# The lane of the other half's mixer is stepped at 1.15 pieces a step instead of 3

## The chip, the cores and the metric

The kernel runs on one core of one Trainium2 chip. The metric is the device time of one execution in microseconds; lower is better. All values are float32, and the large products run as three passes over numbers split into two parts of reduced mantissa (`float32r`).

## The reference

The reference is a decoder trunk of two layers over 1024 tokens of width 1024. Each layer has a mixer of three parallel head groups, a channel MLP and a gated per-layer embedding:

```python
xn = rmsnorm(h, attn_norm_g)
z = xn @ w_in
za, zq, zk, zv, zc = split(z)
ya = chunk_gmlp(za, ...)             # gated MLP over chunks of 128 tokens
yb = swa_sink_attention(q, k, zv)    # 8 query heads, 2 kv heads, window 128
yc = s5_ssm(zc, ...)                 # state space groups, scanned over time
y = concat([rmsnorm(ya), rmsnorm(yb), rmsnorm(yc)])
h = h + y @ w_out
h = h + square(relu(rmsnorm(h) @ w_ff1)) @ w_ff2     # D_FF = 4096
gate = sigmoid(rmsnorm(h) @ w_ple_gate)
h = h + gate * (p_i @ w_ple_proj)
```

## The kernel before

The 1024 tokens are cut into two halves of 512 (half 0 and half 1). Every product has 512 tokens as its moving side and 128 channels as its stationary side; a column block with 8 blocks of depth takes 8 times 3 passes = 24 matmuls. Weights come by DMA in float32 (512 KB each) and are split into a high part by ScalarE (line 104) and a low part by VectorE (line 105) before TensorE can use them; `Ring` loads them ahead of use, two tiles ahead for the MLP's ring (three buffers), one ahead for the mixer's ring (two buffers).

The main work is `window(l, h)`, once for each layer and half, in the order (0,0), (0,1), (1,0), (1,1): the MLP in 8 chunks of 512 hidden channels, then the 8 gate products of the embedding. A chunk has 4 up products (24 matmuls each, line 359 through `cm`; eviction by lines 1344 to 1348 into the tile `A`), then 8 down products of 12 matmuls each, added to `H` in `f2` (line 1333). In the last chunk `f2` also sums squares and makes the split input `x` for the gates (lines 329, 89, 90). After it `rstd_wide` makes the norm `rbc` (matmul line 288, a chain of VectorE and ScalarE steps on lines 289 to 297, PSUM bank "o", of which there is one), and the gates' evictions (line 1390) need it. The gates may use six banks ("mm" two, "s" two, "x", "p") before the first must be free again.

While the window of one half is written, a second generator, the lane, writes the mixer of the other half: `project` (z products: token part line 710, channel part through `cm` into bank "s"), `attention`, `ssm`, `gmlp` and `mix_out` (8 column blocks through `cm` into bank "s", added to `H` on line 1310, then its own `rstd_wide` and the split of the next MLP's input `x`). A piece is what the lane's generator does up to its next `yield`. `main` runs the window's own generator, and each 12 matmuls of it make a step: `tick` adds the lane's rate to an account and runs one piece for each whole unit in it. Two more ticks stand by hand in the first pair of down products of each chunk. So a chunk has 8 + 2 + 6 = 16 steps, the 8 gates have 16, and a window has 144; 120 of them stand before `until` in the last chunk, where all lanes are run on until the other half's `attention` and `ssm` are written. After the window `finish` writes what is left of the lane.

From the generators, a lane of `mix_lane` has 25 pieces in `project`, 42 or 43 in `attention` (half 0 or 1), 34 in `ssm`, 18 in `gmlp` and 18 in `mix_out`: 137 or 138. The lane in the first window is `left_lane`, of which `attention`, `ssm`, `gmlp` with the preparation of layer 1, and `mix_out` fall there; it has no `project`. The last window has no lane.

The order in which the pieces are written is not the order in which an engine runs them. The kernel leaves the order on each engine to the compiler's scheduler, which simulates the program, and at each point takes, of the instructions that it holds to be ready on an engine, the one that was written first. Each engine then runs its instructions in the order so fixed. The rate of a lane is therefore its precedence: a lane written at 3 pieces a step stands, as a whole, ahead of all of the MLP from the third chunk on.

Of the kernel before, what the change touches and what calls it, by code (L numbers as in the profile page):

```python
# [38 lines left out]
PASSES = ((0, 0), (1, 0), (0, 1))  # L39


RATE, RATE0, RATEL = 3.0, 2.0, 3.0


class Ring:
# [17 lines left out]
class Trunk:  # L63
# [1415 lines left out]
    def run(self):  # L1479
        self.setup()  # L1480
        zws, self.zw = ExitStack(), None
        self.zw = self.pool(zws, "zw", 4, side=self.side(0), reuse_waits="tile")
        xs, xp = self.stage("xin", 0)
        left = self.lane(self.left_lane(), RATEL)
        for _ in self.first_x(0, xp, left):
            pass
        x1 = self.lane(self.first_x(1, xp))
        gen = self.project0()
        z0 = self.lane(gen)
        self.until(lambda: x1[3] and ("zq", 0, 0) in self.flags)  # L1490
        xs.close()
        self.until(lambda: {"zg", "rotary"} <= self.flags)
        zws.close()
        self.lanes.remove(z0)
        pzs = ExitStack()
        self.zpools.append(self.pool(pzs, "pz", 2, side=self.side(0), reuse_waits="tile"))
        self.lane(self.gmlp(0, 0, 0, "x", [("attn", 0, 0)]), RATE0)
        self.until(lambda: True)
        self.lane(self.attention(0, 0, 0), RATE0)
        self.main(gen)  # L1500
        self.main(self.embed())
        self.until(lambda: {("attn", 0, 0), ("gm", 0, 0)} <= self.flags)
        self.zpools.pop()
        pzs.close()
        self.finish(self.lane(self.mix_out(0, 0, self.fring, "mm", 3)))
        seq = [(l, h) for l in range(DEPTH) for h in range(2)]
        nxt = left
        for i, (l, h) in enumerate(seq):
            self.window(l, h, self.stages(*seq[i + 1]) if i + 1 < len(seq) else set())
            if i + 1 < len(seq):  # L1510
                self.finish(nxt)
            if i + 2 < len(seq):
                nxt = self.lane(self.mix_lane(*seq[i + 2]), RATE)
# [30 lines left out]
```

## Time and profile before

| | |
|---|---|
| median of 3 runs | 2381.09 us |
| profiled execution: its own time | 2385.95 us |
| profiled execution: span | 2384.2 us |
| TensorE matmul busy | 2325.3 us (98%) |
| TensorE weight load busy | 1885.4 us (79%) |
| VectorE busy | 1552.8 us (65%) |
| ScalarE busy | 1027.8 us (43%) |
| granted TensorE clock, mean | 0.99 |

The runs shown are 2380.5, 2381.09 and 8480.06 us; the median is used. Busy times are unions of the instructions of one engine; a matmul's end is modelled, so neighbouring matmuls overlap in the records and their spacing is read from their starts.

### The profile page before, as it was taken

What the parts mean: (1) busy time and instruction counts of PE and PEld (TensorE: products, weight loads), DVE (VectorE), ACT (ScalarE), POOL (GpSimd) and SP (SyncE); (2) the same over time, 40 slices, a digit from 0 to 9 for tenths busy, and PEclk for the clock granted to TensorE, in tenths of its full rate; (3) what the DMA queues carried; (4) which work ended last, traced back from release to release, by engine and by line L of the source; (5) the groups of instructions that cost most, each with busy time, mean ns of one, the idle gap of its engine ahead of it and who ended that gap; (6) DMA issues with size and microseconds to landing.
All of it is one profiled execution on the core that took longest, in us unless ns stands there. A gap on an engine that the chain in (4) does not pass through costs nothing.

```text
span 2384.2 us, 29265 instructions
## 1 busy us (share of the span) xinstructions
PE 2325.3 (98%) x10941; PEld 1885.4 (79%) x10941; DVE 1552.8 (65%) x2700; ACT 1027.8 (43%) x1787; POOL 5.4 (0%) x15
## 2 busy tenths in 40 slices
PE   7998899999999999999999999999999999999998
PEld 5886687788788887777888888777888887888887
DVE  7877767675966765676585774676657674444455
ACT  7427646433334443553342543464334343322333
POOL 0000000000000000000000000000000000000000
PEclk9998999999999999999999999999999999999999
DMA  8663632253553335324443344522534334333333
GB/s 244 188 203 119 208 99 64 80 173 106 145 156 102 111 125 155 95 78 140 123 135 124 98 145 124 145 72 76 166 105 135 124 97 134 97 96 94 94 97 98
DMA packets 403558, 295.94 MB, mean 124 GB/s; under 512 B 66668, under 2 KB 376024, under 8 KB 401624
## 3 DMA queue, kind: packets, MB, share of 16 engines
q1 hardware_dynamic: 403416, 294.07, 41.1%
q8 instruction: 86, 1.41, 0.3%
q14 instruction: 56, 0.46, 0.1%
HBM read 250.48 MB, written 43.54 MB: 123 GB/s over the span
## 4 chain that ended last, share of the span: by engine, by line
PE 83%; DMA 7%; DVE 5%; ACT 3%; issue 2%; SPq 1%; ACTq 0%; DVEq 0%
PE mm_ps L359 43%; PE x_ps L359 20%; PE s_ps L359 8%; DMA st<-in_w_in 2%; DVE w L105 2%; PE s_ps L710 1%; PE po L1259 1%; PE pss L1201 1%; ACT w L104 1%; PE p_ps L359 1%; DMA st<-in_w_out 1%; PE p_ps L947 1%; DMA yu<-ye 1%; PE pt L1238 1%; SPq L98 1%
## 5 line engine op out<-in xcount | busy, mean ns | idle before, releaser
L104 ACT CAST w<-st 128x1024 fp32r<-128x1024 f32 x364 | 387.9, 1067 | 853.1 <-PE mm_ps L359 430.0
L359 PE MATMUL mm_ps<-x,w 128*128 128x512 f32 x2904 | 708.4, 396 | 7.9 <-ACT x L89 4.2
L359 PEld LDWEIGHTS mm_ps<-x,w 128*128 128x128 f32 x2904 | 544.5, 190 | 133.0 <-issue 10.1
L105 DVE TENSOR_TENSOR w<-st,w 128x1024 fp32r<-128x1024 f32 x364 | 448.5, 1234 | 202.6 <-ACT w L104 191.6
L359 PE MATMUL mm_ps<-A,w 128*128 128x512 f32 x2016 | 500.8, 392 | 2.5 <-DVE H L1333 2.5
L359 PEld LDWEIGHTS mm_ps<-A,w 128*128 128x128 f32 x2016 | 375.7, 188 | 85.4 <-DVE H L1333 4.9
L359 PE MATMUL x_ps<-A,w 128*128 128x512 f32 x1056 | 272.8, 393 | 4.1 <-DVE H L1333 4.1
L359 PE MATMUL x_ps<-x,w 128*128 128x512 f32 x1104 | 272.2, 394 | 0.0
L359 PE MATMUL s_ps<-x,w 128*128 128x512 f32 x1056 | 252.4, 391 | 4.8 <-DVE w L105 2.6
L359 PEld LDWEIGHTS x_ps<-x,w 128*128 128x128 f32 x1104 | 205.6, 188 | 45.6 <-issue 3.4
L359 PEld LDWEIGHTS s_ps<-x,w 128*128 128x128 f32 x1056 | 198.1, 188 | 49.1 <-DVE w L105 4.0
L359 PEld LDWEIGHTS x_ps<-A,w 128*128 128x128 f32 x1056 | 196.5, 188 | 51.0 <-DVE H L1333 8.3
L1333 DVE TENSOR_TENSOR H<-H,mm_ps 128x512 f32<-128x512 f32 x168 | 113.2, 683 | 84.2 <-PE mm_ps L359 83.3
L1344 DVE SCALAR_TENSOR_TENSOR r<-mm_ps,rbc 128x512 f32<-128x512 f32 x88 | 60.7, 690 | 119.2 <-PE mm_ps L359 119.2
L710 PE MATMUL s_ps<-w,x 128*128 128x512 f32 x384 | 101.3, 404 | 4.1 <-ACT x L89 2.6
L1333 DVE TENSOR_TENSOR H<-H,x_ps 128x512 f32<-128x512 f32 x88 | 60.2, 684 | 68.8 <-PE x_ps L359 68.2
L1348 DVE TENSOR_TENSOR A<-q,A 128x512 fp32r<-128x512 f32 x128 | 87.8, 686 | 6.8 <-ACT q L1347 6.6
L710 PEld LDWEIGHTS s_ps<-w,x 128*128 128x128 f32 x384 | 73.6, 194 | 20.8 <-ACT x L89 3.0
L1346 ACT ACTIVATE A<-r 128x512 fp32r<-128x512 f32 x128 | 80.2, 627 | 8.1 <-DVE r L1344 7.9
L1347 ACT ACTIVATE q<-r 128x512 f32<-128x512 f32 x128 | 78.9, 617 | 0.0
L1224 ACT ACTIVATE pr<-pr,anm,hf 128x128 f32<-128x128 f32 x128 | 61.6, 485 | 17.4 <-DVE anm L1221 17.4
L89 ACT ACTIVATE x<-H,gT 128x512 fp32r<-128x512 f32 x80 | 53.7, 711 | 13.5 <-PE s_ps L359 7.7
(386 smaller groups left out, 2112.3 us busy)
## 6 DMA issues: line engine op xcount, KB each, us to landing
st<-in_w_ff SPq DMA_DIRECT2D x256, 512.0 KB, 4.1
st<-in_w_out SPq DMA_DIRECT2D x32, 512.0 KB, 4.1
st<-in_w_ple_gate SPq DMA_DIRECT2D x32, 512.0 KB, 4.1
st<-in_w_in SPq DMA_DIRECT2D x18, 512.0 KB, 4.4
p<-par SPq DMA_DIRECT2D x8, 1024.0 KB, 8.5
pj<-pjz SPq DMA_DIRECT2D x32, 256.0 KB, 2.2
H<-hs SPq DMA_DIRECT2D x4, 2048.0 KB, 7.9
pj<-pj SPq DMA_DIRECT2D x32, 256.0 KB, 3.4
```

Source lines behind the costliest of these rows:

```text
L89: self.S.activation(hi, x, AF.Copy, scale=g)
L98: self.Q.dma_start(sv[:, :, c0:c1], src)
L104: self.S.copy(hi, src)
L105: self.V.tensor_tensor(lo, src, hi.bitcast(F32), ALU.subtract)
L359: self.T.matmul(ps, w[:, i, k, c0:c0 + P], X[:, j, k, :], start=(start and n == 0), stop=(stop and n == last))
L710: T.matmul(pss[b], X[:, j, 2 * s + kk, c], w[:, i, kk, :], start=(s == 0 and kk == 0 and n == 0), stop=(s == 3 and kk == 1 and n == 2))
L1224: S.activation(pr[:, i], pr[:, i], AF.Exp, bias=nm[:, i:i + 1], scale=f[:, i:i + 1], accum_out=den[:, i:i + 1])
L1333: V.tensor_tensor(H[:, m], H[:, m], ps, ALU.add)
L1344: V.scalar_tensor_tensor(r, ps, 0.0, self.R[h][1], ALU.max, ALU.mult)
L1346: S.activation(A[:, 0, m], r, AF.Square)
L1347: S.activation(q, r, AF.Square)
L1348: V.tensor_tensor(A[:, 1, m], q, A.bitcast(F32)[:, 0, m], ALU.subtract)
```

## The change

One rate is changed and one is added. `RATE`, the rate of `mix_lane` in the windows (0,1) and (1,0), goes from 3.0 to 1.15. The lane of the first window, created with `RATEL` = 3.0 and used at 3.0 so far, is set to the new `RATEW` = 1.25 before the first window is written. `RATE0` and `RATEL`, and with them the part before the first window, stay. The setting of the scheduler stays.

```diff
-RATE, RATE0, RATEL = 3.0, 2.0, 3.0
+RATE, RATEW, RATE0, RATEL = 1.15, 1.25, 2.0, 3.0
...
         seq = [(l, h) for l in range(DEPTH) for h in range(2)]
         nxt = left
+        nxt[1] = RATEW
         for i, (l, h) in enumerate(seq):
             self.window(l, h, self.stages(*seq[i + 1]) if i + 1 < len(seq) else set())
```

No instruction is added or removed by it, and no tile or buffer changes its size.

## Rows read from the trace of the kernel before

**Rows 1.** The page: busy time of the engines, and the granted clock in 40 slices

```profile
PE 2325.3 (98%) x10941; PEld 1885.4 (79%) x10941; DVE 1552.8 (65%) x2700; ACT 1027.8 (43%) x1787; POOL 5.4 (0%) x15
...
PEclk9998999999999999999999999999999999999999
```

**Rows 2.** Busy time by stretch: before the windows, then the four windows

```profile
core 0: us, PE busy (x) PEld busy (x) DVE busy (x) ACT busy (x) POOL busy (x), PEclk, DMA share, GB/s
0.00:338.00 338.00, 306.17 (x1525) 245.40 (x1525) 250.71 (x658) 188.06 (x410) 2.51 (x12) 0.96 0.61 184
338.00:842.10 504.10, 499.01 (x2375) 403.25 (x2375) 359.63 (x592) 222.97 (x383) 0.95 (x1) 0.99 0.39 115
842.10:1405.30 563.20, 557.03 (x2620) 452.37 (x2619) 369.46 (x602) 242.84 (x409) 0.96 (x1) 1.00 0.40 120
1405.30:1967.30 562.00, 557.40 (x2636) 452.90 (x2635) 369.70 (x599) 241.24 (x408) 0.95 (x1) 1.00 0.39 118
1967.30:2384.20 416.90, 405.73 (x1792) 331.45 (x1790) 203.26 (x253) 132.67 (x178) 0.00 (x0) 0.99 0.34 101
```

**Rows 3.** Busy time by stretch of 25 us: starts of lanes, attention, the lone MLP

```profile
350.00:375.00 25.00, 21.81 (x104) 18.41 (x103) 19.91 (x40) 17.07 (x43) 0.00 (x0) 0.86 0.25 74
925.00:950.00 25.00, 22.05 (x96) 17.35 (x96) 20.23 (x38) 10.07 (x16) 0.00 (x0) 1.00 0.59 156
950.00:975.00 25.00, 22.80 (x98) 18.57 (x99) 11.03 (x16) 8.39 (x14) 0.00 (x0) 0.93 0.49 149
1000.00:1025.00 25.00, 25.00 (x135) 19.41 (x134) 18.30 (x43) 15.12 (x44) 0.00 (x0) 1.00 0.29 84
2050.00:2075.00 25.00, 25.00 (x112) 20.70 (x111) 11.78 (x14) 6.23 (x7) 0.00 (x0) 1.00 0.35 106
```

**Rows 4.** Chain that ended last, in order of time: start, us, what (lone MLP)

```profile
2096.34 5.44 PE mm_ps L359 x24
```

**Rows 5.** Timeline of TensorE where lanes start: start, us, instruction [idle before <-releaser]

```profile
358.72 0.66 PE L1188 MATMUL pq<-identr,qst 128*128 128x128 f32 x4 [1.79 <-ACT kT L1122]
360.06 1.32 PE L1201 MATMUL pss<-kT,qt 128*128 128x256 f32 x8 [0.68 <-ACT qt L1191]
362.86 2.08 PE L1201 MATMUL pss<-kT,qt 128*128 128x256 f32 x8 [0.73 <-ACT qt L1191]
...
925.96 5.96 PE L359 MATMUL s_ps<-x,w 128*128 128x512 f32 x25 [1.00 <-DVE hss L701]
933.33 5.50 PE L359 MATMUL s_ps<-x,w 128*128 128x512 f32 x23 [1.41 <-DVE w L105]
939.62 0.47 PE L359 MATMUL s_ps<-x,w 128*128 128x512 f32 x1 [0.57 <-DVE z L742]
964.75 0.77 PE L1120 MATMUL pk<-identr,kst 128*128 128x128 f32 x4 [2.20 <-DVE kst L1117]
...
1500.20 5.53 PE L359 MATMUL s_ps<-x,w 128*128 128x512 f32 x23 [1.20 <-DVE w L105]
1506.59 0.47 PE L359 MATMUL s_ps<-x,w 128*128 128x512 f32 x1 [0.63 <-DVE z L742]
1530.54 0.66 PE L1120 MATMUL pk<-identr,kst 128*128 128x128 f32 x4 [1.25 <-DVE kst L1117]
```

**Rows 6.** Line 359 alone, by stretch: project, then up to mix_out, two windows

```profile
842.10:955.30 113.20, 67.53 (x281) 51.80 (x279) 1.00 0.48 143
955.30:1286.30 331.00, 292.20 (x1224) 228.38 (x1224) 0.99 0.37 113
1405.30:1522.20 116.90, 72.58 (x304) 56.30 (x302) 1.00 0.49 145
1522.20:1864.40 342.20, 300.80 (x1271) 235.95 (x1271) 1.00 0.37 111
```

**Rows 7.** Timelines of TensorE and VectorE at the end of window (1,0)

```profile
1924.80 1.02 PE L288 MATMUL o_ps<-nacc,onesr 128*128 128x512 f32 x2
1942.91 1.02 PE L288 MATMUL o_ps<-nacc,onesr 128*128 128x512 f32 x2
1956.02 5.60 PE L359 MATMUL p_ps<-x,w 128*128 128x512 f32 x24
...
1928.17 0.74 DVE L90 SCALAR_TENSOR_TENSOR x<-H,gT,x 128x512 fp32r<-128x512 f32 x1
1954.49 0.69 DVE L1390 TENSOR_TENSOR gt<-p_ps,rbc 128x512 f32<-128x512 f32 x1
```

**Rows 8.** Timeline of VectorE at the end of window (0,1): the lane's last split

```profile
1341.66 0.76 DVE L90 SCALAR_TENSOR_TENSOR x<-H,gT,x 128x512 fp32r<-128x512 f32 x1
```

**Rows 9.** Timeline of TensorE inside windows: waits for the MLP's own eviction

```profile
597.47 3.02 PE L359 MATMUL x_ps<-A,w 128*128 128x512 f32 x12 [1.15 <-DVE H L1333]
1718.96 5.76 PE L359 MATMUL mm_ps<-A,w 128*128 128x512 f32 x24 [1.19 <-DVE H L1333]
```

## The prediction

> **What bounds the kernel now.** I read first the busy times of the page, then the same by stretch with a boundary at each window, then the stretches of 25 us inside the windows, and where one of those is not full, the timeline of TensorE. The reader is to see the same thing at each level: TensorE has work nearly all of the time. It is busy for 98% of the span, VectorE for 65%, ScalarE for 43% [rows 1]. In the four windows it is idle for 5.1, 6.2, 4.6 and 11.2 us [rows 2]; the last of these has no lane, so the change can't reach it. Since ends of matmuls are modelled, busy time alone does not say that TensorE is at its peak, so I take a stretch in which the MLP runs alone: 112 matmuls in 25 us, 24 of them in 5.44 us, or 226.7 ns each [rows 3, 4]. The stretches with a lane reach this spacing too, and the mixed attention stretch, with its shorter matmuls, is busy for 25.00 of 25 us at a granted clock of 1.00 [rows 3]. So what an order can win is what the windows lose at a few places, and those places are at the start of each lane: 3.2 us of waiting in window (0,0), 5.2 us in (0,1), 3.1 us in (1,0) [rows 5], the first two followed by a spell at half clock (1.2 GHz): a mean of 0.86 over 25 us costs 3.5 us, 0.93 costs 1.75 us [rows 3].
>
> **What is removed, added and moved.** Nothing is computed anew: the 10941 matmuls, the weight splits and the DMAs are the same, so the edit's own work costs 0. What moves is precedence. Written at 3 pieces a step, a lane of 137 pieces is written in 46 of a window's 144 steps and is ahead of nearly all of the MLP. It does not run there. In window (0,1) line 359 starts 281 matmuls up to the end of `project`, of which 96 are `project`'s own, so 185 are the MLP's: 15.4 steps of 12; then 1224, or 102 steps, until `mix_out` begins. In (1,0) it is 304 - 96 = 208 (17.3 steps) and 1271 (105.9 steps) [rows 6]. So `project` runs its 25 pieces at 1.62 and 1.44 pieces a step, and `attention`, `ssm` and `gmlp`, 94 or 95 pieces, at 0.92 and 0.90. Their own chain of dependences sets that, since nothing stands ahead of them.
>
> Against these numbers the new rate can be read. At 1.15 pieces a step `project` needs 25 / 1.15 = 21.7 steps where it took 15.4 and 17.3. A step of the MLP is 12 x 226.7 ns = 2.72 us [rows 4], so `project` ends 6.3 x 2.72 = 17.2 us later in (0,1) and 4.4 x 2.72 = 12.0 us later in (1,0). After it 1.15 is above 0.9: the lane falls behind the place where it is written, is then again the older work, and goes at its own pace. So the whole lane, `mix_out` too, ends 12 to 17 us later. What hides that: the lane's last split of the next window's input is done at 1342.4 and no later than 1928.9, the next windows begin at 1405.3 and 1967.3 [rows 2, 7, 8], so there are 62.9 and 38.4 us to spare. Cost 0; if that cover were gone, each microsecond would cost one. In (0,0) the lane has no `project`, 1.25 is above 0.9 as well, and its end does not move. DMAs of the mixer's weights move with their pieces; their ring is paced by the matmuls that free its buffers, as before.
>
> What is gained is at the lane's start. A piece of `project` now has 12 / 1.15 = 10.4 MLP matmuls beside it where it had 12 / 1.62 = 7.4; a weight tile of two pieces thus gets 6 x 0.2267 = 1.4 us more to be split before its first matmul. The five waits of `project`'s last blocks are 1.00, 1.41, 0.57, 1.20 and 0.63 us [rows 5], none longer than that: I take all of them, 4.8 us. The waits of the first steps of `attention` (2.20 and 1.25 us for `kst`, 3.2 us in (0,0)) and the half-clock spells (5.25 us) [rows 3, 5] are chains in which each step waits for the one before; more MLP matmuls in between cover some of them. Bounds are nothing and 11.9 us; between these I take half, 5.9 us. Against that stands what a new order brings by itself: two waits of 1.15 and 1.19 us inside windows, where the MLP's eviction was late behind lane work on VectorE [rows 9]. No row shows how many the new order will have; the bounds are none and, from the last two windows' total of such idle time, about 5 us each. I take one more in each of (0,1) and (1,0), 2.3 us.
>
> Sum against the profiled execution: 2385.95 - 4.8 - 5.9 + 2.3 = 2377.5 us. The median is 2381.09 / 2385.95 = 0.998 of that execution, so 2373 us.
>
> One rule speaks against mixing the streams for longer. The attention stretch, as mixed as any, kept its clock at 1.00, and the spell of 3.5 us came after idle time [rows 3]. The Trainium skill (TensorE: Matmul & The Clock Gate, Loop structure matters more than you think) asks that a loop's matmuls follow one another at once and that waits between bursts be kept out, lest the clock fall; by that, one more spell of 3.5 us in each of three windows would make the sum 2388 us. The trace bears out only the part about waits.
>
> **The rivals.** A, the forecast: 2373 us.
>
> B, nothing happens: the scheduler already spreads the lane over 120 steps by its dependences, and the waits at its start belong to the chain itself and stay. For it speaks 0.9 pieces a step under any precedence; against it that `project` does run faster than 1.15. Time: 2381 us.
>
> C, slower, by a late lane. With less precedence each piece of `attention` to `gmlp` may wait for a turn on TensorE. From 38.4 us of lateness of `mix_out` the lane of (1,0) costs time, from 62.9 us that of (0,1) too. Half a microsecond on each piece makes 12.0 + 95 x 0.5 = 59.5 and 17.2 + 94 x 0.5 = 64.2 us, which cost 21.1 and 1.3 us: 2385.95 + 22.4, times 0.998, is 2404 us. Slower by 2% (47.6 us) needs 0.63 us a piece. Against it: a lane that lags is older than the MLP and goes first.
>
> D, faster by over 2%. Weight loads fill 80.3% of the three windows with a lane (1308.5 of 1629.3 us) [rows 2] and 82.8% of the lone MLP [rows 3]; if the difference were idle TensorE, 1629.3 x (1 - 80.3 / 82.8) = 49 us could be won: 2332 us. The Trainium skill (Trainium Kernel Development and Optimization, Performance Expectations) holds matmul busy time to be a bad measure and weight-load busy time a good one, which is this reading. Against it: the attention stretch has 77.6% with no idle time, because its matmuls are short and many [rows 3].
>
> E, slower within 2%, by the tail. The gates' norm of window (1,0) runs on bank "o" after the lane's: its matmul comes at 1942.9, 18.1 us after the lane's, the first eviction at 1954.5, and the seventh gate, which needs that bank again, starts at 1956.0 [rows 7]: 1.5 us to spare. If the lane's norm comes 12 us later, still just ahead of the gates', TensorE waits 10.5 us, in two windows 21 us: 2377.5 + 21, times 0.998, is 2394 us. For it speaks the shift; against it that the later `mix_out` leaves the last down products, and so the gates' norm, to go before it.
>
> **How the numbers follow.** A 0.47, B 0.23, E 0.15, C 0.08, D 0.03, and 0.04 for mixtures outside them. Predicted: 2373 us. Its own range reaches from all 16.7 us of waits and spells gone (2365 us) to none (2381 us). The range given, 2354 to 2404 us, takes in A, B, E and C as far as priced, and on the low side another 11 us for idle time that the rows of the lane's start do not hold. A measurement of this kernel can tell about 2% from no change; that is below 2333 us and above 2429 us. Faster by over 2% is D alone, 0.03; slower by over 2% is the far part of C, 0.03; the rest, 0.94, is within 2%.
>
> **What would show it.** In the changed kernel: `project` ending some 12 to 17 us later after its window's start, `mix_out`'s last matmul later by as much; about 260 MLP matmuls up to `project`'s end where there were 185 and 208; the waits for `w` (line 105) and `z` (line 742) gone; fewer than three half-clock spells between the first window's start and the last's; the window lengths near 501, 559 and 561 us. Wrong would be: the first stretch of line 359 unchanged (B); a next window whose first up products wait for `x` (C); idle TensorE among the gates before line 1390 (E); windows shorter by 15 us each (D).

## The result, and the profile after

The change made the kernel slower: 2413.12 us (median of 4 runs, 2409.85 to 2417.36) against 2381.48 us for the kernel before, measured beside it. The ratio that goes with the 95% interval is 1.0127 (1.0113 to 1.0141); the two medians alone give 1.0133. That is less than the 2% which the prediction took for a clear change, but the interval lies clear of 1. The 2381.48 us are the median of four runs, of which one took 8480.06 us. The forecast was 2373 us in a range up to 2404 us: the time moved the other way and lies outside the range.

In every row of the kernel after, line numbers are one higher than before, since the diff adds a line at the top: line 359 is now 360, 288 is 289, 1310 is 1311, 1333 is 1334, 105 is 106. The gates' evictions, 1390, are 1391. The page of the profiled execution (2417.36 us) answers to [rows 1]:

```profile
span 2415.6 us, 29271 instructions
PE 2334.8 (97%) x10941; PEld 1891.6 (78%) x10941; DVE 1554.8 (64%) x2700; ACT 1028.1 (43%) x1787; POOL 5.4 (0%) x15
PEclk9998999999999999999999989999999989999999
```

The work is the same, matmul for matmul, and the span is 31.4 us longer than 2384.2. Two digits 8 are new: the granted clock dips once near 0.58 and once near 0.82 of the span. To find where the 31.4 us went I cut the span where each window's work begins, 0.3 us before the first eviction of an up product. These are the three windows with a lane, first before and then after, with the columns of [rows 2]; the last two rows of the second fence are short stretches at the ends of windows (0,1) and (1,0).

```profile
363.00:854.60 491.60, 490.12 (x2330) 396.18 (x2331) 352.66 (x582) 215.42 (x368) 0.95 (x1) 1.00 0.39 117
854.60:1417.90 563.30, 557.13 (x2621) 452.44 (x2620) 370.75 (x603) 242.75 (x409) 0.96 (x1) 1.00 0.39 118
1417.90:1987.70 569.80, 564.23 (x2676) 458.12 (x2675) 367.23 (x593) 241.75 (x407) 0.95 (x1) 1.00 0.40 120
```

```profile
361.40:852.50 491.10, 489.32 (x2329) 394.92 (x2328) 351.54 (x580) 216.10 (x370) 0.95 (x1) 1.00 0.38 115
852.50:1429.40 576.90, 560.97 (x2631) 456.33 (x2630) 372.15 (x603) 243.30 (x409) 0.95 (x1) 0.99 0.39 118
1429.40:2017.70 588.30, 571.49 (x2674) 462.75 (x2673) 369.81 (x597) 242.01 (x408) 0.95 (x1) 0.98 0.39 116
1395.30:1409.00 13.70, 5.04 (x13) 3.81 (x12) 11.03 (x17) 4.92 (x8) 0.00 (x0) 0.51 0.24 73
1972.10:1989.20 17.10, 7.78 (x16) 4.99 (x17) 13.17 (x22) 4.34 (x7) 0.00 (x0) 0.51 0.20 61
```

Window (0,0) is 0.5 us shorter, (0,1) 13.5 us longer and (1,0) 18.5 us longer: 31.5 us together, which is all of it. The short stretches show what the ends of those windows hold: at a clock of 0.51, which is the lower of the two levels (1.2 GHz), TensorE is busy for 5.04 of 13.7 us and for 7.78 of 17.1 us. So the next views are the timelines of TensorE and VectorE there. On TensorE (start, us, instruction, count, idle time before it and its releaser):

```profile
1314.54 0.96 PE L360 MATMUL mm_ps<-x,w 128*128 128x512 f32 x3 [0.68 <-DVE x L91]
1316.41 0.50 PE L360 MATMUL mm_ps<-x,w 128*128 128x512 f32 x1 [0.90 <-DVE x L91]
1317.61 7.09 PE L360 MATMUL p_ps<-x,w 128*128 128x512 f32 x24 [0.70 <-DVE rs_a L297]
...
1361.70 16.26 PE L360 MATMUL s_ps<-x,w 128*128 128x512 f32 x71
1383.25 1.02 PE L289 MATMUL o_ps<-nacc,onesr 128*128 128x512 f32 x2
1385.25 5.60 PE L360 MATMUL x_ps<-x,w 128*128 128x512 f32 x24
1394.38 1.12 PE L289 MATMUL o_ps<-nacc,onesr 128*128 128x512 f32 x2 [3.53 <-DVE rs_a L297]
1404.17 8.07 PE L360 MATMUL mm_ps<-x,w 128*128 128x512 f32 x24 [8.66 <-DVE gt L1391]
1412.08 5.60 PE L360 MATMUL s_ps<-x,w 128*128 128x512 f32 x24
...
1894.67 7.43 PE L360 MATMUL x_ps<-x,w 128*128 128x512 f32 x19 [0.76 <-DVE w L106]
1962.27 1.02 PE L289 MATMUL o_ps<-nacc,onesr 128*128 128x512 f32 x2
1972.76 2.08 PE L289 MATMUL o_ps<-nacc,onesr 128*128 128x512 f32 x2 [3.57 <-DVE rs_a L297]
1983.49 8.53 PE L360 MATMUL p_ps<-x,w 128*128 128x512 f32 x24 [8.66 <-DVE gt L1391]
```

and on VectorE, in window (0,1):

```profile
1316.27 0.69 DVE L330 TENSOR_TENSOR nacc<-nacc,nsq 128x512 f32<-128x512 f32 x1
...
1372.99 0.68 DVE L1311 TENSOR_TENSOR H<-H,s_ps 128x512 f32<-128x512 f32 x1
1378.22 0.69 DVE L330 TENSOR_TENSOR nacc<-nacc,nsq 128x512 f32<-128x512 f32 x1
1393.65 0.68 DVE L297 SCALAR_TENSOR_TENSOR rs_a<-rs_a,o_ps 128x512 f32<-128x512 f32 x1
1395.54 0.70 DVE L290 TENSOR_SCALAR o_ps<-o_ps 128x512 f32<-128x512 f32 x1 [0.49 <-PE o_ps L289]
1402.61 0.69 DVE L298 SCALAR_TENSOR_TENSOR rbc<-rs_a,rbc 128x512 f32<-128x512 f32 x1
1403.33 0.69 DVE L1391 TENSOR_TENSOR gt<-mm_ps,rbc 128x512 f32<-128x512 f32 x1
```

Read together, they tell this. The MLP's last down products are done early, and the squares for the gates' norm (line 330) are complete at 1316.27 + 0.69 = 1316.96. Yet that norm's matmul runs at 1394.38, 77.4 us later. In between the lane's `mix_out` ends (last addition to `H` at 1372.99, last square at 1378.22), its own norm matmul runs on bank "o" at 1383.25, and its chain reads that bank until 1393.65 + 0.68 = 1394.33. There is one bank "o", and `mix_out`'s `rstd_wide` is written ahead of the gates'. The gates' products, meanwhile, have filled their six banks; TensorE waits 3.53 us, issues the gates' norm, waits 8.66 us for the first gate eviction at 1403.33, and then runs 24 matmuls in 8.07 us where full clock takes 5.60. In (1,0) the same pattern stands from 1962.27 to 1983.49 + 8.53: 3.57 and 8.66 us, and 8.53 us for 24 matmuls. In the kernel before, the two norm matmuls lie 30 us apart in (0,1) and 18 us in (1,0) [rows 7], and TensorE waits for neither; these are the two of (0,1):

```profile
1344.01 1.02 PE L288 MATMUL o_ps<-nacc,onesr 128*128 128x512 f32 x2
1374.53 1.02 PE L288 MATMUL o_ps<-nacc,onesr 128*128 128x512 f32 x2
```

The 13.5 us of (0,1) can be added up from such rows. At the end 3.53 + 8.66 + (8.07 - 5.60) = 14.7 us. At 1314 to 1318, where `gmlp` and the last chunk's tail share VectorE, 0.68, 0.90 and 0.70 us of waiting and 7.09 us for a block of 5.60: 3.8 us. Against this the lane's start lost 5.2 us of waits [rows 5] and 1.6 us to the clock before (25 matmuls from 965.32 on took 7.47 us, where 24 x 0.2267 + 0.39 = 5.83 is full speed), and now 1.45 us: -5.4 us. Sum: 13.1. For (1,0) it is 3.57 + 8.66 + (8.53 - 5.60) + (2.08 - 1.02) = 16.2 us; waits of 0.32, 1.13 and 0.76 us near 1891 with 19 matmuls behind them, most at half clock (7.43 us instead of about 4.46): 5.2 us; less the 3.1 us of waits at the start of the lane [rows 5], all gone: 18.3 us of 18.5. The new 1.15 us wait inside a window is in place of one of [rows 9].

### The profile page after: what moved, and what is told of

The parts are those of the page before. It is cut to its first block, busy times and chain, and to the rows that moved or that the text cites. A ratio compares the mean times of both kernels' runs of the same rounds, so it can differ in the third digit from the quotient of the medians.

```text
span 2415.6 us, 29271 instructions
## 1 busy us (share of the span) xinstructions
PE 2334.8 (97%) x10941; PEld 1891.6 (78%) x10941; DVE 1554.8 (64%) x2700; ACT 1028.1 (43%) x1787; POOL 5.4 (0%) x15
## 3 DMA queue, kind: packets, MB, share of 16 engines
q8 instruction: 86, 1.41, 0.2%
```

## The experiments

Two things had to be told apart, and then sized: whether the loss is the order in which bank "o" is handed out (theory T), or that `mix_out` holds both banks "s" so that the gates fill the rest whatever their norm does (S), or that the mixer's matmuls stand ahead of the gates' on TensorE whatever the bank (L); and which part of the lane's lower precedence makes it late. The times of each of (0,1) and (1,0) below are counted from that window's first up eviction. The kernel before was measured again beside each group of runs, at 2383.64, 2383.27 and 2382.93 us, and each ratio is to that. Before, the first query step of the lane's `attention` comes at +123.2 and +130.0 us, `mix_out`'s last addition to `H` at +480.4 and +495.0. After, it is +151.0 and +153.5, and +520.2 and +520.9.

**Another bank for the gates' norm, in the kernel after.**

```diff
-        self.rstd_wide(tail, D, EPS, h, (fp, "r", 2))
+        self.rstd_wide(tail, D, EPS, h, (fp, "r", 2), "t")
```

> The changed kernel with one edit: the norm of the gates takes PSUM bank t instead of bank o, so that it no longer shares a bank with the norm of the lane's mix_out. Theory T (the single bank o is handed out in the order written, so the gates' norm stands behind mix_out's, and TensorE runs dry at the end of the windows (0,1) and (1,0)): the two waits of 3.5 and 8.7 us in each of the two windows and the half-clock spells after them go, 2372 to 2386 us. Rival S (mix_out holds both banks s, so that the gates have four banks of six and fill them whatever their norm does): the waits stay, 2403 to 2415 us. Rival L (the mixer's matmuls stand in TensorE's order ahead of the gates', bank or no bank): 2403 to 2415 us.

Measured: 2374.26 us, ratio to before 0.9955 (0.9939 to 0.9972). TensorE, VectorE and the two stretches:

```profile
1315.63 1.13 PE L289 MATMUL t_ps<-nacc,onesr 128*128 128x512 f32 x2
...
1381.45 1.02 PE L289 MATMUL o_ps<-nacc,onesr 128*128 128x512 f32 x2
1388.44 5.38 PE L360 MATMUL mm_ps<-x,w 128*128 128x512 f32 x23
```

```profile
1327.89 0.69 DVE L1391 TENSOR_TENSOR gt<-mm_ps,rbc 128x512 f32<-128x512 f32 x1
```

```profile
852.90:1412.30 559.40, 557.72 (x2637) 454.81 (x2636) 369.85 (x603) 242.27 (x408) 0.95 (x1) 1.00 0.41 121
1412.30:1976.40 564.10, 560.25 (x2659) 455.04 (x2658) 368.38 (x597) 242.51 (x410) 0.95 (x1) 1.00 0.40 121
```

The lane is as late as in the kernel after (+518.8 and +520.7 us for the last addition), but the gates' norm, on bank "t", now runs 66 us ahead of `mix_out`'s, the first gate is evicted at 1327.89, and the gates run at full speed behind `mix_out` (23 matmuls in 5.38 us). Windows (0,1) and (1,0) are 559.4 and 564.1 us, 3.9 and 5.7 us shorter than before, at a clock of 1.00. So with the bank out of the way neither the lateness nor the mixing costs anything here.

**The same edit in the kernel before.** The diff is the same.

> The kernel before with the same edit, the norm of the gates on bank t. Theory T: before, the first gate bank came free 1.5 us before it was needed, so there is nothing to win, 2376 to 2384 us. Rival (the edit itself is worth something in any order, so that a gain in the run with the changed rates says nothing of the rates): 2340 to 2370 us.

Measured: 2381.06 us, 0.9992 (0.9983 to 1.0002), and the two windows as they were:

```profile
849.30:1412.90 563.60, 557.27 (x2620) 452.73 (x2620) 370.75 (x603) 242.45 (x409) 0.96 (x1) 1.00 0.39 118
1412.90:1983.50 570.60, 564.01 (x2675) 458.31 (x2675) 367.37 (x593) 241.36 (x407) 0.96 (x1) 1.00 0.40 120
```

The bank is worth nothing by itself. What the kernel with both edits gains (2374.26 against 2381.06, about 7 us) comes from the lower rate.

**The order instead of the bank, in the kernel after.** Both norms stay on "o", but in layer 1's `mix_out` the norm is written after the gates'.

```diff
         self.rstd_wide(tail, D, EPS, h, (fp, "r", 2))
+        self.flags.add(("gn", l, h))
...
+        if l:
+            yield from self.wait(("gn", h, 1 - h))
```

> The changed kernel with both norms on bank o as they are, but mix_out's norm is written after the gates' norm in the windows (0,1) and (1,0). Theory T (the bank goes to the norms in the order in which they are written): the gates' norm no longer stands behind mix_out's, and the time is that of the run with bank t, 2368 to 2382 us. Rival S (the bank is short as such, two norms at one time cost whichever comes first): 2395 to 2415 us.

Measured: 2373.06 us, 0.9961 (0.9949 to 0.9973); windows of 559.6 and 564.8 us. TensorE has the gates' norm first and the lane's 66 us later, in one bank:

```profile
1313.20 1.13 PE L289 MATMUL o_ps<-nacc,onesr 128*128 128x512 f32 x2
...
1379.04 1.02 PE L289 MATMUL o_ps<-nacc,onesr 128*128 128x512 f32 x2
```

One bank is enough: what counts is who is written first. With the run on "t" this shows that the bank is handed out in the order written, not to whoever is ready first.

**Low precedence for `project` alone.** RATE stays 1.15, and is set to 3.0 behind `project`.

```diff
-                nxt = self.lane(self.mix_lane(*seq[i + 2]), RATE)
+                nxt = self.mixe = self.lane(self.mix_lane(*seq[i + 2]), RATE)
...
         yield from self.project(l, h, self.mring, "s")
+        self.mixe[1] = 3.0
```

> The changed kernel in which the lane of the windows (0,1) and (1,0) has rate 1.15 for project alone and 3.0 from then on. If the lateness of mix_out comes from project as the prediction had it (12 to 17 us), mix_out ends as late as in the changed kernel (38 us) and the time is 2405 to 2415 us. If the stages after project are slowed by their precedence, mix_out ends only some 11 us late, the gates' norm is held up by less, and the time is 2381 to 2394 us.

Measured: 2414.05 us, 1.0126 (1.0111 to 1.0141). The first query step comes at +146.9 and +153.3 us, the last addition at +520.8 and +521.8, the windows take 577.3 and 588.7 us: near the kernel after in every number, the 4 us at the first query step apart. The second branch, 11 us of lateness, did not come; the whole loss comes with the low rate of `project`.

**Low precedence for the rest alone.** RATE 3.0, and 1.15 behind `project`.

```diff
-RATE, RATEW, RATE0, RATEL = 1.15, 1.25, 2.0, 3.0
+RATE, RATEW, RATE0, RATEL = 3.0, 1.25, 2.0, 3.0
...
         yield from self.project(l, h, self.mring, "s")
+        self.mixe[1] = 1.15
```

> The changed kernel with the lane at rate 3.0 for project and 1.15 from then on. If the stages after project are slowed by their precedence: mix_out ends 20 to 30 us late and the gates' norm is held up, 2393 to 2412 us. If they run at their own pace under any rate, as the prediction had it: mix_out ends where it ended before and the time is 2376 to 2386 us.

Measured: 2377.53 us, 0.9969 (0.9958 to 0.9981); +124.3 and +127.7 us, +486.1 and +491.7 us, windows of 564.4 and 566.5 us. The last addition is 5.7 us later than before in one window and 3.3 us earlier in the other: behind `project` the stages of these two windows go nearly at their own pace, as the prediction had it.

**The same with the gates' norm on bank "t".**

> Rate 3.0 for project, 1.15 from then on, and the gates' norm on bank t. If the gain of the run with bank t over the kernel before comes from project being thinned out (its waits for weights and evictions at its end), it is smaller here than there: 2374 to 2380 us. If it comes from the later stages' lower precedence, it is as large: 2368 to 2376 us.

Measured: 2379.97 us, 0.999 (0.998 to 1.0); windows of 560.5 and 568.3 us. With the bank out of the way, a lower rate for the whole lane gains 0.45% and one for all but `project` 0.1%, which puts the gain with `project`. But the run before this one gains 0.31% without `project` and with bank "o", and in the profiles the two windows of this run are 5.5 us shorter than those of the kernel before with bank "t", and those of the run with 1.15 throughout another 5.3 us. So how the gain divides between `project` and the rest is not shown. Nor is it explained that this run is slower than the one before it: its two windows are 2 us shorter together, the difference lies ahead of them, and that part of the span varies between profiles (356 to 363 us to the first up eviction).

**A late `mix_out` at full precedence, in the kernel before.** `mix_out` is written only when the last chunk's down products begin.

```diff
+                self.flags.add(("last", l, h))
...
+        yield from self.wait(("last", h, 1 - h))
         yield from self.mix_out(l, h, self.mring, "s")
```

> The kernel before, rate 3.0 throughout, with one edit: mix_out of the lanes in the windows (0,1) and (1,0) is not written before the last chunk's down products, all earlier stages stay as they were. Theory T (a mix_out that comes after the chunk's tail holds the gates' norm up, whatever made it late): waits before the gates' norm and its evictions as in the changed kernel, 2395 to 2418 us. Rival P (the lower precedence of the lane's earlier stages costs the time in its own right): 2377 to 2390 us, as before.

Measured: 2396.65 us, 1.0062 (1.0045 to 1.0079). `mix_out` ends at +499.7 and +504.2 us, the windows take 567.5 and 574.6 us, 4.2 and 4.8 us longer than before. TensorE at the end of (1,0), where this kernel's line 1391 is the gates' eviction:

```profile
1937.57 1.02 PE L288 MATMUL o_ps<-nacc,onesr 128*128 128x512 f32 x2
1951.59 1.02 PE L288 MATMUL o_ps<-nacc,onesr 128*128 128x512 f32 x2
...
1961.81 8.42 PE L359 MATMUL p_ps<-x,w 128*128 128x512 f32 x24 [6.69 <-DVE gt L1391]
```

Nothing of the lane's start is changed here, and 9 us of lateness in (1,0) bring a wait of the same kind (6.69 us, and 24 matmuls in 8.42 us behind it). There lateness is enough, whatever makes it. In (0,1), 19 us late, no such wait comes: the longest at that window's end is 1.26 us for a weight, and its 4.2 us are not explained.

**How much, by size: RATE 1.5.**

```diff
-RATE, RATEW, RATE0, RATEL = 1.15, 1.25, 2.0, 3.0
+RATE, RATEW, RATE0, RATEL = 1.5, 1.25, 2.0, 3.0
```

> The changed kernel with RATE 1.5 instead of 1.15. project ran at 1.62 and 1.44 pieces a step before, so it is held back by some 1.3 steps (3.5 us) in window (0,1) and not at all in (1,0). Theory T with lateness made in project: mix_out comes ahead of the chunk's tail in (1,0) and about there in (0,1), 2374 to 2392 us. If any rate that thins project out brings the whole cost: 2405 to 2415 us.

Measured: 2393.46 us, 1.0048 (1.003 to 1.0065), just above what was expected; +137.8 and +134.7 us, +499.7 and +503.3 us, windows of 569.1 and 573.0 us. `mix_out` ends as late as in the run before this one, where it was written late at rate 3.0, and the loss is of that size: 10.2 us against 13.4. In (1,0) the wait for the gates' first eviction is 6.69 us in both, and in the next run too, at 8.3, 9.2 and 7.1 us of lateness: it does not grow with the lateness there.

**Low precedence for `project`'s token part alone.** RATE 1.15 as in the kernel after, set to 3.0 between the two parts of `project`.

```diff
-                nxt = self.lane(self.mix_lane(*seq[i + 2]), RATE)
+                nxt = self.mixe = self.lane(self.mix_lane(*seq[i + 2]), RATE)
...
         self.z_roots(l, h, ss)
+        self.mixe[1] = 3.0
         for m in range(4):
```

> The changed kernel in which the lane of the windows (0,1) and (1,0) has rate 1.15 for the token part of project (16 pieces) and 3.0 from its channel part on. If the lane is late because the first steps of attention no longer overlap the channel part (they are written behind it, and it is drawn out), they overlap again here: attention's first query step is less than 12 us late, mix_out too, 2376 to 2394 us. If thinning the token part alone sets the lateness: mix_out is 30 us late or more, 2402 to 2415 us.

Measured: 2387.38 us, 1.0026 (1.0014 to 1.0037); +133.3 and +133.6 us, +494.1 and +502.1 us, windows of 563.5 and 572.5 us. Of the lateness of the first query step 10.1 of 27.8 and 3.6 of 23.5 us stay, of that of the last addition 13.7 of 39.8 and 7.1 of 25.9 us. The larger part belongs to the channel part of `project` and what meets it.

## Why the prediction was wrong

**The step that failed: what hides the later `mix_out`.** The prediction measured its slack against the beginning of the next window, 62.9 and 38.4 us, and put the cost at 0. But the first thing due behind `mix_out` is not the next window: it is the gates' norm, which gets bank "o" only after `mix_out`'s norm. In [rows 7] that left 1.5 us by the prediction's count, from the start of the eviction at 1954.49, and 0.8 us from its end. With that cover gone, each window lost 13.5 and 18.5 us net, and the runs with the bank or the order changed take it all back.

**Rival E had the place, at 0.15, and its "against" was wrong.** It said that a later `mix_out` would leave the gates' norm to go before it. Half of this happened: the down products did go first, the last of their additions (line 1333) ending at 1312.1 instead of 1363.7 in (0,1) and at 1887.4 instead of 1924.6 in (1,0). But what was ready first could not go first. The prediction knew that the order written decides who is taken; it did not carry this over to a buffer of which there is one. Its price, 10.5 us of waiting a window, was near the rows by luck: it was lateness less slack, 12 - 1.5, and the rows have 3.53 + 8.66 = 12.2 us and 3.57 + 8.66 = 12.2 us at 39.8 and 25.9 us of lateness. It left out the matmuls behind the wait, the first of them at half clock: 2.5 and 2.9 us more.

**The lateness was mis-sized: 12 to 17 us forecast, 26 to 40 measured.** Up to the end of the channel part the working held. This is line 360 alone, from the window's start to the end of `project`, in (0,1) and (1,0), and then TensorE there; the first fence answers to [rows 6]:

```profile
843.00:969.30 126.30, 82.55 (x353) 65.81 (x352) 1.00 0.48 143
1411.60:1543.00 131.40, 89.10 (x381) 71.32 (x380) 1.00 0.48 140
```

```profile
930.48 3.04 PE L360 MATMUL s_ps<-x,w 128*128 128x512 f32 x12 [1.45 <-DVE hss L702]
933.36 2.88 PE L360 MATMUL x_ps<-A,w 128*128 128x512 f32 x12
936.08 2.88 PE L360 MATMUL s_ps<-x,w 128*128 128x512 f32 x12
```

353 - 96 = 257 and 381 - 96 = 285 matmuls of the MLP run beside `project`, where about 260 were forecast and 185 and 208 ran before; 12 of the one and 12 of the other alternate. Counted from the window's first up eviction, the channel part's last matmul starts at 115.7 us in (0,1) and 111.8 us in (1,0), where it was 100.2 and 103.6: 15.5 and 8.2 us later, for 17.2 and 12.0 forecast.

What was not seen is what follows. Before, the matmuls of `attention`'s key steps (line 1120) began 8 us ahead of the end of the channel part in both windows (946.8 against 955.1, 1514.0 against 1521.8); after, they begin 12.5 and 12.8 us behind it (981.0 against 968.5, 1554.3 against 1541.5). These are the first of them in (0,1), before and after:

```profile
946.80 0.45 PE L1120 MATMUL pk<-identr,kst 128*128 128x128 f32 x3
...
980.96 0.56 PE L1121 MATMUL pk<-identr,kst 128*128 128x128 f32 x4
```

With this lost overlap the first query step is 27.8 and 23.5 us late. At the other end, in (0,1), `gmlp` now meets the last chunk's tail on VectorE and takes 72.8 us instead of 53.7, and `mix_out` ends 39.8 us late (25.9 in (1,0)). So a delay at the front of a chain of stages did not stay the same: it grew where a stage lost its overlap or met another one's peak. The run with only the token part slowed bears this out; how the rest divides between key steps and `gmlp` is read from the traces and was not isolated. In (0,0), where 0 was forecast, the last addition of `mix_out` starts at 764.1 instead of 738.3. The lane has no `project` there; its `attention` takes 140.9 us from its first query step to the last scaling of its outputs, where it took 121.0, so under 1.25 it did not keep its pace, and why was not isolated. It cost nothing: the gates' norm of that window comes later still, at 809.6 (807.1 before), and the window's length did not change.

**The gain came out near its size.** The waits of `project` and of the first key steps in (0,1) and (1,0) are gone, save the 1.45 us for `hss` above. At the start of (0,0) they are not: 2.01 and 0.67 us are left of 3.2, at a mean clock of 0.93 from 350 to 375 us where it was 0.86, and the window, forecast at 501 us, takes the 504.1 us of [rows 2] again. With the bank out of the way the lower rate gives 2381.06 - 2374.26 = 6.8 us, where 4.8 + 5.9 - 2.3 = 8.4 us were forecast. No run changes `RATEW` alone, and no run sizes these terms one by one. The windows forecast at 559 and 561 us are cut as in [rows 2] (563.2 and 562.0 before); by first up evictions, that run has 3.9 and 5.7 us less than before in them. That `attention` and `ssm` run at a rate of their own, not the lane's, held in (0,1) and (1,0) and not in (0,0).

**The other rivals.** B: not so, since `project` did move. C: the lane was late, but the next window did not wait for it. D: the weight loads of (0,1) and (1,0) fill no more of the time than before, 456.33 of 576.9 and 462.75 of 588.3 us. A spell at half clock for the mixing itself, which gave 2388 us, did not come: in the run with bank "t" the streams are mixed as long and the clock is 1.00 in both windows. What the Trainium skill (TensorE: Matmul & The Clock Gate, Loop structure matters more than you think) says of waits between bursts agrees with the trace: after 8.66 us of waiting the next 24 matmuls took 8.07 us, not 5.60, the first of them at a granted clock of 0.50.

## What to carry to other kernels

When a stream is given less precedence, list every buffer that it shares with the others and of which there is only one, and see who gets it behind it: slack is measured to the first of these, not to the place where the stream's output is read. A delay at the front of a chain of stages can grow on its way (here from 15.5 to 39.8 and from 8.2 to 25.9 us), so its size at the end is not the size of the edit. And when the trace shows a wait for another stream's normal work (here for `rs_a`) far from where it is used, the order of a buffer is the thing to look at; a second buffer or an order written the right way gave the gain without the loss: 2374.26 and 2373.06 us here, faster than both kernels.

## What the hardware showed

The lower clock cost less than its spell is long. In the 13.7 us at a clock of 0.51, 8.66 us were idle anyway, and the loss was 2.5 us on the 24 matmuls behind them. Nor did a long wait have to come first: near 1891 us waits of 0.32, 1.13 and 0.76 us were followed by 19 matmuls that took 7.43 us, at a granted clock of 0.50 from 1893.9 to 1900.4. In [rows 5] waits of 1.00, 1.41 and 0.57 us between 925 and 950 us left the clock at 1.00 [rows 3], so the length of single waits does not tell these cases apart.
